# Dealing the row blocks of four matrices over the partitions in turn, in a batched matmul

## The chip, the cores and the metric

The kernel runs on one core of a Trainium2 chip. Time is the device time of one execution in microseconds (us), the median over several executions. A profile also gives TensorE's granted clock, the share of its full clock that it was allowed to run at (1.00 is all of it), and the span, which is the time that the profile covers.

## The reference

```python
b1, b2, m, k, n = 8, 16, 256, 512, 384
x      = randn(b1, b2, m, k)      # float32, 67.1 MB
weight = randn(b1, b2, k, n)      # float32, 100.7 MB
out    = matmul(x, weight)        # float32, 50.3 MB
```

That is 128 separate products of 256x512 by 512x384. Each input is used once, so 218.1 MB have to pass through the DMA queues whatever the kernel does.

## The kernel before

The kernel handles four matrices (G = 4) at a time, 32 groups in all. One load brings the 1,024 rows of four x matrices to 128 partitions, eight consecutive rows (16 KB) to each. With C = 32, partitions 32i to 32i+31 hold matrix i.

```python
e.dma_start(                                   # load
    x_sb[s % XS][:],
    x_rows[bass.ds(n * (G * M), G * M)].rearrange("(p r) k -> p r k", r=R),
).then_inc(x_in[s % XS], 16)
for d in range(G // D):                        # two weight loads of 1.5 MB follow
    ...
```

ScalarE casts x to bf16. TensorE transposes it in pairs of bf16 words, so that in `x_t` the 128 columns (one per partition of x) stand two elements apart. VectorE casts the weights and copies the transposes out of PSUM, the memory that TensorE writes to. Then four matmuls run on four column strips of 32, one for each matrix, each with the 32 columns of its matrix as the stationary operand, which a weight load (LDWEIGHTS in the profile, 4,096 of them beside 4,096 matmuls) brings in before the matmul:

```python
for ko in range(KO):
    for i in range(G):
        mine = slice(i * C, (i + 1) * C)
        ins = e.matmul(
            po[(s * T + q) % PO][mine, rr, :N],
            x_t[s % TS][:, 2 * q + rr, ko // 2, mine, ko % 2],   # stationary
            w_bf[(s * G + i) % WBS][:, ko, :],                   # moving
            start=(ko == 0), stop=(ko == KO - 1),
        )
```

All loads and stores are issued by one queue (SP). Buffers hold two groups of x and of weights and four of the output.

## Time and profile before

| | before |
|---|---|
| time, median | 519.93 us (519.65 to 520.08) |
| DMA packets' share of 16 engines | 99.2% |
| rate in the middle | 425 to 431 GB/s |
| TensorE / VectorE / ScalarE busy | 61% / 62% / 41% |
| one group of four matrices | 15.97 us |

### The profile page before, as it was taken

The numbers are of one execution on the slowest core, as the hardware profiler recorded it, in microseconds if no ns is written. First come the engines' busy times: TensorE is split into PE (matmuls) and PEld (weight loads), VectorE is DVE, ScalarE is ACT, GpSimd is POOL, SyncE is SP. The second block draws the span as 40 slices with busy tenths as digits, with TensorE's granted clock in tenths as the row PEclk, the third lists the DMA queues.
The fourth block names the chain that finished last, engine by engine and source line by source line (L and its number), as shares of the span: only waits on it lengthen the run. The fifth ranks groups of instructions, "written<-read, shape, count | busy, mean of one in ns | idle before, by whom it ended". The sixth has DMA issues, their size and how long they took to land.

```text
span 518.3 us, 11239 instructions
## 1 busy us (share of the span) xinstructions
PE 315.5 (61%) x4608; PEld 198.8 (38%) x4608; DVE 323.9 (62%) x384; ACT 212.7 (41%) x193; POOL 0.7 (0%) x6
## 2 busy tenths in 40 slices
PE   0686773576655675655756557665567665675653
PEld 0455452343433443433424334343344333443331
DVE  0878867655577555775556765557755577555670
ACT  3065462454234553245542445423454324553242
POOL 0000000000000000000000000000000000000000
PEclk9988788877687778678776877778787868886787
DMA  8999999999999999999999999999999999999995
GB/s 332 431 426 426 427 427 429 430 426 429 430 428 429 431 426 428 428 431 431 425 429 429 430 430 429 427 428 429 430 430 428 426 431 430 429 428 427 428 431 214
DMA packets 18868, 218.16 MB, mean 421 GB/s; under 512 B 2096, under 2 KB 2096, under 8 KB 2608
## 3 DMA queue, kind: packets, MB, share of 16 engines
q1 hardware_dynamic: 18864, 218.11, 99.2%
q8 instruction: 2, 0.03, 0.0%
q14 instruction: 2, 0.02, 0.0%
HBM read 167.77 MB, written 50.33 MB: 421 GB/s over the span
## 4 chain that ended last, share of the span: by engine, by line
DMA 81%; DVE 12%; issue 2%; PE 2%; ACT 1%; SPq 0%; DVEq 0%; ACTq 0%
DMA w_sb<-in_weight_dram 81%; DVE w_bf L148 12%; PE po L181 2%; ACT x_bf L130 0%; DVEq _compat.py:109 0%; SPq L108 0%; ACT out_sb L195 0%; SPq L100 0%; DVE x_t L154 0%; DVEq L143 0%; DVEq L230 0%; SPq L107 0%; ACTq L194 0%; SPq L288 0%; SPq L54 0%
## 5 line engine op out<-in xcount | busy, mean ns | idle before, releaser
L148 DVE CAST w_bf<-w_sb 64x1536 bf16<-64x1536 f32 x256 | 244.5, 955 | 179.4 <-DMA w_sb<-in_weight_dram 166.7
L181 PE MATMUL po<-w_bf,x_t 128*32 128x384 bf16 x4096 | 231.4, 400 | 121.0 <-DVE x_t L154 121.0
L195 ACT COPY out_sb<-po 128x768 f32<-128x768 f32 x128 | 99.2, 802 | 290.2 <-PE po L181 290.2
L181 PEld LDWEIGHTS po<-w_bf,x_t 128*32 128x32 bf16 x4096 | 124.5, 117 | 225.4 <-DVE x_t L154 130.9
L167 PE MATMUL pt<-identity,x_bf 128*128 128x128 f32 x512 | 84.0, 329 | 73.0 <-ACT x_bf L130 73.0
L130 ACT CAST x_bf<-x_sb 128x2048 bf16<-128x2048 f32 x64 | 118.4, 1901 | 6.1 <-DMA x_sb<-in_x_dram 6.1
L167 PEld LDWEIGHTS pt<-identity,x_bf 128*128 128x128 f32 x512 | 74.3, 213 | 84.9 <-issue 84.9
L154 DVE COPY x_t<-pt 128x1024 bf16<-128x1024 bf16 x128 | 79.5, 683 | 1.0
L130 ACT ACT_TABLE_LOAD x1 | 1.3, 1283 | 1.3 <-PEq L237 1.3
masks.py:199 POOL TENSOR_SCALAR_AFFINE_SELECT identity<-identity 128x128 f32<-128x128 f32 x1 | 0.3, 292 | 0.2 <-POOL identity L204 0.2
L204 POOL MEMSET identity<- 128x128 f32 x1 | 0.2, 204 | 0.5 <-SPq L54 0.5
L277 POOL MEMSET const-bfloat16-1.0<- 128x1 bf16 x1 | 0.1, 101 | 0.0
L277 POOL MEMSET const-uint8-127<- 128x1 uint8 x1 | 0.1, 101 | 0.0
L277 POOL MEMSET const-float32-0.0<- 128x1 f32 x1 | 0.1, 98 | 0.2 <-issue 0.2
L277 POOL MEMSET const-float32-1.0<- 128x1 f32 x1 | 0.1, 98 | 0.0
## 6 DMA issues: line engine op xcount, KB each, us to landing
w_sb<-in_weight_dram SPq DMA_DIRECT2D x64, 1536.0 KB, 27.5
x_sb<-in_x_dram SPq DMA_DIRECT2D x32, 2048.0 KB, 25.8
out_dram<-out_sb SPq DMA_DIRECT2D x31, 1536.0 KB, 30.6
out_dram<-out_sb SPq DMA_DIRECT2D x4, 384.0 KB, 3.6
```

The source lines that it names most:

```text
L130: ins = e.copy(out=x_bf[s % BS][:, :, h], in_=x_sb[s % XS][:].rearrange("p r (q s c) -> p r s q c", s=S, c=KO)[:, :, h],)
L148: e.tensor_copy(out=w_bf[(s * G + d * D + a) % WBS][h * HP : (h + 1) * HP], in_=w_sb[slot][a * HP : (a + 1) * HP, h * KO : (h + 1) * KO, : ...
L154: e.tensor_copy(out=x_t[s % TS][:, 2 * q : 2 * q + 2], in_=pt[(s * T + q) % PT][:].bitcast(bf16),).then_inc(t_copied, 1)
L167: ins = e.transpose(pt[(s * T + q) % PT][:, rr, h, :], words[:, 2 * q + rr, h :: KO // 2], identity[:],)
L181: ins = e.matmul(po[(s * T + q) % PO][mine, rr, :N], x_t[s % TS][:, 2 * q + rr, ko // 2, mine, ko % 2], w_bf[(s * G + i) % WBS][:, ko, :], ...
L195: e.copy(out=out_sb[s % OS][:, 2 * q : 2 * q + 2, :], in_=po[(s * T + q) % PO][:, :, :N],).then_inc(o_copied, 1)
L204: e.memset(identity[:], 0.0).then_inc(id_done, 1)
L277: nc = _bacc.Bacc("TRN2", target_bir_lowering=False, num_devices=1)
```

## The change

The change deals the row blocks out in turn: partition 4c + i gets block c of matrix i. Every run of four partitions then holds one block of each of the four matrices, and one load reads from four places in HBM at once. So that the results stay in place, a matmul now picks every fourth column. Presumably it was meant to spread the reads.

```diff
         e.dma_start(
-            x_sb[s % XS][:],
-            x_rows[bass.ds(n * (G * M), G * M)].rearrange("(p r) k -> p r k", r=R),
+            x_sb[s % XS][:].rearrange("p r k -> p (r k)"),
+            x_rows[bass.ds(n * (G * M), G * M)].rearrange(
+                "(i c r) k -> c i (r k)", i=G, r=R
+            ),
         ).then_inc(x_in[s % XS], 16)
@@ multiply
-                            x_t[s % TS][:, 2 * q + rr, ko // 2, mine, ko % 2],
+                            x_t[s % TS][:, 2 * q + rr, ko // 2, i::G, ko % 2],
```

## The prediction

> **What bounds the kernel now.** I read the page from the DMA side first, because it has the largest shares: the 40-slice table, the queue table, and the chain that ended last.
>
> ```profile
> DMA  8999999999999999999999999999999999999995
> GB/s 332 431 426 426 427 427 429 430 426 429 430 428 429 431 426 428 428 431 431 425 429 429 430 430 429 427 428 429 430 430 428 426 431 430 429 428 427 428 431 214
> ...
> q1 hardware_dynamic: 18864, 218.11, 99.2%
> ...
> DMA 81%; DVE 12%; issue 2%; PE 2%; ACT 1%; SPq 0%; DVEq 0%; ACTq 0%
> ```
>
> The second row is the rate in each fortieth of the span (13 us): a ramp at 332, a flat 425 to 431 GB/s, a tail at 214. The queue line says that packets filled 99.2% of 16 engines' 518.3 us. The chain agrees: 81% of it is a transfer. The transfers are not late for want of requests: in the table of issues a weight load lands 27.5 us after it is issued, although its 1.5 MB at 429 GB/s need 3.7 us. So about 27 us of work is queued ahead of it.
>
> No view lists single packets, so I summed the trace's packet records by size. There are 4,096 packets of 16 KB, which are the x loads (32 loads x 128 partitions), with a median of 611 ns and a 99th percentile of 627 ns. There are 12,160 packets of 12 KB (weights and stores) with a median of 460 ns. Per engine that is 157.7 us for x, 351.4 us for 12 KB packets, 3.9 us for the last stores' 3 KB packets and 1.2 us for semaphores: 514.2 us of 518.3. The time is this sum plus a start and an end.
>
> Next the compute side, in the groups by line and in one group of the timeline (columns there: start, length, engine, line, work, count, idle before):
>
> ```profile
> L181 PE MATMUL po<-w_bf,x_t 128*32 128x384 bf16 x4096 | 231.4, 400 | 121.0 <-DVE x_t L154 121.0
> L181 PEld LDWEIGHTS po<-w_bf,x_t 128*32 128x32 bf16 x4096 | 124.5, 117 | 225.4 <-DVE x_t L154 130.9
> ```
>
> ```profile
> 254.25 7.86 DVE L148 CAST w_bf<-w_sb 64x1536 bf16<-64x1536 f32 x8 [5.55 <-DMA w_sb<-in_weight_dram]
> ...
> 255.66 3.11 PE L167 MATMUL pt<-identity,x_bf 128*128 128x128 f32 x16 [1.98 <-ACT x_bf L130]
> ...
> 262.14 2.48 DVE L154 COPY x_t<-pt 128x1024 bf16<-128x1024 bf16 x4
> 262.88 0.14 PEld L181 LDWEIGHTS po<-w_bf,x_t 128*32 128x32 bf16 x8 [4.52 <-DVE x_t L154]
> 262.89 7.28 PE L181 MATMUL po<-w_bf,x_t 128*32 128x384 bf16 x128 [4.12 <-DVE x_t L154]
> ...
> 266.70 3.07 PEld L181 LDWEIGHTS po<-w_bf,x_t 128*32 128x32 bf16 x76 [0.16 <-issue]
> ```
>
> A group of four matrices takes 15.97 us (in the chain the weight casts start at 206.39, 238.33 and 270.27, two groups apart). VectorE waits 5.55 us for the weights' DMA, then PE waits for VectorE. Were data always there, PE's loop would be 3.1 (transposes) + 0.75 (first copy, 262.14 to 262.89) + 7.3 (matmuls) = 11.2 us, VectorE's 7.9 + 2.5 = 10.3 us. Compute has 4.8 us to spare per group.
>
> One thing in the last row matters later: 76 weight loads in 3.07 us are one per 40 ns, back to back. In that stretch (granted clock 0.99) weight loading is full; earlier in the same phase (clock 0.50) four loads fill 0.16 of every 0.32 us.
>
> [...] Before, both sides count 128. After, the source counts 32 (c) outermost and the destination 128[...]. No run here shows the new shape yet.[...] The new x load puts successive partitions 512 KiB apart[...]. The transposed x columns were read at a 4 B step[...] and will be read at 16 B[...]. The trace of before has no such read, so it cannot confirm the penalty.
>
> **The change part by part.**
> *x load.* It removes nothing: 32 loads of 2 MB, still one contiguous 16 KB row block per partition, so still 4,096 packets of 16 KB. What moves is which block each partition gets: partition 4c+i now has block c of matrix i, where partition 32i+c had it. Only the HBM addresses change. Cost per engine: 256 packets x 611 ns = 156.4 us, unchanged if the memory keeps up. Before, the engines read blocks of the same 2 MB, only in another order, and 99% of the packets were within 16 ns of the floor; HBM showed no strain. I take an allowance of 0 to 3 ns per packet in the mean, 256 x 3 = 0.8 us at most, centre 0.3 us. The three-dimensional source may cost SP a little more at each issue than the present 0.33 us, but behind a 27 us backlog only the very first issue shows: 0.2 us as a guess.
>
> *Matmuls.* Same number of instructions in the same order on every engine (I compared the two builds), same 32 columns and 384 moved elements. The picked columns come out as matrix i's rows in order, so the output rows and stores are as before. Only the weight-load step grows.[...] I bound it: at worst[...] the pace doubles, from 40 to an estimated 80 ns. In the slow-clock part four loads then need just the 0.32 us there are: no change. In the fast part 0.16 us per four becomes 0.32 us. A steady group gets 76 x 40 ns = 3.0 us longer: 11.2 + 3.0 = 14.2 us, still under 15.97. Nothing of that reaches the end time.
>
> *The tail.* This is the one place where matmul time is on the path. The chain of waits ends with:
>
> ```profile
> 502.57 6.94 PE po L181 x128
> ```
>
> After it come one 0.80 us copy and one 384 KB store. 88 of its 128 weight loads run at the fast pace (3.66 us in the timeline); at 80 ns they take 7.0 us, so +3.4 us on the end; with half of the penalty (60 ns) it is +1.6 us. I give no penalty, half and the whole equal chances: (0 + 1.6 + 3.4)/3 = +1.7 us expected, less some 0.5 us because the stores of the last groups, still queued until about 511 us, hide a part of it: +1.2 us.
>
> Sum: 519.9 + 0.3 (HBM) + 0.2 (first issue) + 1.2 (tail) = 521.6; the outcome without any penalty, 520.4, is the most probable single one, so I settle a little lower, at 521.2.
>
> **The rivals.**
> *A: PE takes over as the bound.* The matmul phase may grow to 15.97 - 3.1 - 0.75 = 12.1 us, that is 95 ns per weight load, before the DMA queue starves. For: the loads are already back to back at 40 ns. Against: they would have to slow 2.4-fold. At 120 ns a group would take 3.85 + 128 x 0.12 = 19.2 us, and 32 groups some 615 us. Chance 3%.
>
> *B: HBM slows the x packets.* For: four streams 512 KiB apart[...]. Against: each read is still 16 KB long,[...] and the packet times of before sit on their floor with one core alone on its memory.[...] At 10%, 536 us. Chance of over 2% from here: 2%.
>
> *C: the engines share the work worse*[...]. For: a new shape that the trace hasn't shown.[...] With x at half rate: +157 us, 677 us. Chance 2%.
>
> *D: it gains.* Spreading x over four matrices could be meant to feed HBM better. Against:[...] Over 2% would need 10.4 us; 1% as a chance for a cause not thought of.
>
> **How range and chances follow.** Unchanged kernels repeat within 519.65 to 520.08. Below 519 only rival D leads. Upwards, a doubled weight load gives about 523.8[...]. So 519.0 to 525.0 should hold it 8 times in 10. Rivals A, B and C sum to 0.07 for slower by over 2% (above 530); rest 0.92.
>
> **What would show each step right or wrong.** Right: the GB/s row again at 425 to 431 with q1 near 99%, 4,096 packets of 16 KB with a median of 611 ns, and VectorE still waiting for the weights' DMA before each other group. The weight-load rows of the timeline tell the step's price: 0.16 us per four means no penalty, up to 0.32 us in the fast part the penalty, and the last matmul phase would read 6.9 us or up to 10.3 us. Wrong: a GB/s row that falls (B or C; packets slower everywhere is B, uneven or doubled ones C), or DMA tenths below 9 in the middle with VectorE waiting for PE (A).

## The result

The changed kernel takes 520.36 us (520.20 to 520.53, four runs) against 519.98 us. The ratio is 1.0009 with a 95% interval of 0.9994 to 1.0024. A ratio is the mean time of one kernel's fast runs over that of the other's in the same rounds, so it is not quite the ratio of the medians quoted beside it.

The profile after, first the table of slices, the queue line and the chain by engine:

```profile
DMA  8999999999999999999999999999999999999995
GB/s 337 427 427 426 418 428 429 435 424 429 428 427 431 428 427 430 429 428 431 426 429 426 432 430 427 426 431 429 428 430 431 427 429 431 428 428 426 429 430 219
...
q1 hardware_dynamic: 18864, 218.11, 99.1%
...
DMA 80%; DVE 12%; issue 2%; PE 2%; ACT 1%; SPq 0%; DVEq 0%; ACTq 0%
```

Little moved here. The one slice that stands out is the fifth, with 418 GB/s where the kernel before has 427; more on it below. In the packet records, the 4,096 packets of 16 KB are still there, with a median of 611 ns as before. The sums per engine are 157.1 us for x (157.7 before), 351.7 us for the 12 KB packets (351.4), 3.9 and 1.2 us for the rest: 513.9 us against 514.2. Which engine moved a packet is not recorded: "per engine" means the sum divided by 16.

The groups by line (busy us, mean ns of one, idle time before and its releaser):

```profile
L183 PE MATMUL po<-w_bf,x_t 128*32 128x384 bf16 x4096 | 238.5, 408 | 122.4 <-DVE x_t L156 122.4
L183 PEld LDWEIGHTS po<-w_bf,x_t 128*32 128x32 bf16 x4096 | 157.6, 148 | 200.3 <-DVE x_t L156 130.4
```

The mean weight load has gone from 117 to 148 ns and weight-load busy time from 124.5 to 157.6 us. This is the largest visible price of the change, 33 us of work, and the time does not show it. The same group of the timeline as before (start, length, engine, line, work, count, idle before):

```profile
254.45 7.86 DVE L150 CAST w_bf<-w_sb 64x1536 bf16<-64x1536 f32 x8 [5.43 <-DMA w_sb<-in_weight_dram]
...
256.36 2.84 PE L169 MATMUL pt<-identity,x_bf 128*128 128x128 f32 x16 [1.99 <-ACT x_bf L132]
...
262.34 2.48 DVE L156 COPY x_t<-pt 128x1024 bf16<-128x1024 bf16 x4
263.09 7.36 PEld L183 LDWEIGHTS po<-w_bf,x_t 128*32 128x32 bf16 x128 [4.29 <-DVE x_t L156]
263.09 7.70 PE L183 MATMUL po<-w_bf,x_t 128*32 128x384 bf16 x128 [3.89 <-DVE x_t L156]
```

VectorE still waits over 5 us for the weights, and TensorE for VectorE. The weight loads now merge into one row of 7.36 us, where before they stood as blocks of 0.16 us. Merged rows mislead, though. They join pieces with small gaps between them, and that is how I misread the row "3.07 ... x76" of before. Busy time by window is the honest view. Its columns are the window, its length, then busy us with counts for PE, weight loads, VectorE, ScalarE, GpSimd, then granted clock, DMA share and GB/s. This is one fast stretch before:

```profile
266.70:270.20 3.50, 3.46 (x84) 1.98 (x76) 0.00 (x0) 2.58 (x3) 0.00 (x0) 0.99 1.00 421
```

and the same window after, where the granted clock was 0.84:

```profile
266.70:270.20 3.50, 3.50 (x80) 2.74 (x76) 0.00 (x0) 1.98 (x3) 0.00 (x0) 0.84 1.02 432
```

76 weight loads kept the loader busy for 1.98 of 3.50 us before and 2.74 after. It was never full. The instruction records say why: at the fast clock the four loads of a block start within some 20 ns of each other, last 97 ns each, and the next four start 162 ns after the first four. After the change each lasts 137 ns or a little more, and the blocks are still 162 ns apart. The matmuls set the pace, in both kernels.

The second small difference is on the queue that issues the DMAs. A line of the x tile's view before (durations min/median/max in ns):

```profile
L100 SPq DMA_DIRECT2D x_sb<-in_x_dram x32: 327/333/703, 1.0 to 463.6; - x32
```

and after:

```profile
L100 SPq DMA_DIRECT2D x_sb<-in_x_dram x32: 545/566/661, 1.0 to 464.2; - x32
```

An issue of the new load takes 0.23 us more. 27 us of work are queued, so I expected only the very first issue to matter. The first packet starts at 2.40 us after the span's start instead of 1.99. The packets make up for that at once, though, and lose something later. The same columns as above, first before:

```profile
0.00:4.00 4.00, 0.00 (x0) 0.00 (x0) 0.00 (x0) 1.28 (x1) 0.70 (x6) 1.00 0.55 131
62.00:66.00 4.00, 3.99 (x100) 2.29 (x92) 3.01 (x4) 3.35 (x4) 0.00 (x0) 1.00 0.99 418
```

and after:

```profile
0.00:4.00 4.00, 0.00 (x0) 0.00 (x0) 0.00 (x0) 1.28 (x1) 0.70 (x6) 1.00 0.41 139
62.00:66.00 4.00, 2.62 (x68) 2.08 (x56) 3.15 (x4) 3.93 (x3) 0.00 (x0) 1.00 1.01 390
```

In the first 4 us the changed kernel starts as many bytes as the other, and a few more: the first 64 packets last 717 ns in the mean instead of 859. Between 62 and 66 us it falls behind: the 12 KB packets that start from 62.5 to 65.0 us last 537 ns in the mean instead of 466. Against packets of the usual length (611, 460 and 121 ns), the surplus per engine is 0.5 us smaller than before in the first 8 us, and 0.3 us larger from 60 to 68 us.

The last matmul phase, on the chain that ended last, after the change:

```profile
502.67 7.42 PE po L183 x116
```

It is 0.48 us longer than the 6.94 us of before, yet the span is only 0.06 us longer (518.40 against 518.34). The profiled run of before, at 520.11 us, is one of the slower ones of its kernel, so this is weak evidence that the chain does not set the end. In the packet records of before there is something stronger. 12 KB packets follow each other without a gap until 512.48 us, and 3 KB packets, one each 118 ns, until 516.28. I read this row as one engine that works through its 12 KB store packets and then its 32 packets of 3 KB; the records name no engine. It reaches the last piece only at 515.3 us, although that piece was issued at about 510.4.

### The profile page after: what moved, and what is told of

Read it like the earlier page. It is cut to its first block, busy times and chain, and to the rows that moved or that the text cites. A ratio compares the mean times of both kernels' runs of the same rounds, so it can differ in the third digit from the quotient of the medians.

```text
span 518.4 us, 11239 instructions
## 1 busy us (share of the span) xinstructions
PE 315.7 (61%) x4608; PEld 227.0 (44%) x4608; DVE 323.9 (62%) x384; ACT 213.1 (41%) x193; POOL 0.7 (0%) x6
## 2 busy tenths in 40 slices
DMA packets 18868, 218.16 MB, mean 421 GB/s; under 512 B 2096, under 2 KB 2096, under 8 KB 2608
## 3 DMA queue, kind: packets, MB, share of 16 engines
q1 hardware_dynamic: 18864, 218.11, 99.1%
## 4 chain that ended last, share of the span: by engine, by line
DMA 80%; DVE 12%; issue 2%; PE 2%; ACT 1%; SPq 0%; DVEq 0%; ACTq 0%
DMA w_sb<-in_weight_dram 80%; DVE w_bf L150 12%; PE po L183 2%; ACT x_bf L132 1%; DVEq _compat.py:109 0%; SPq L100 0%; SPq L110 0%; ACT out_sb L197 0%; DVE x_t L156 0%; DVEq L145 0%; SPq L109 0%; DVEq L232 0%; ACTq L196 0%; SPq L290 0%; SPq L54 0%
## 5 line engine op out<-in xcount | busy, mean ns | idle before, releaser
L183 PE MATMUL po<-w_bf,x_t 128*32 128x384 bf16 x4096 | 238.5, 408 | 122.4 <-DVE x_t L156 122.4
L183 PEld LDWEIGHTS po<-w_bf,x_t 128*32 128x32 bf16 x4096 | 157.6, 148 | 200.3 <-DVE x_t L156 130.4
L169 PE MATMUL pt<-identity,x_bf 128*128 128x128 f32 x512 | 77.3, 310 | 71.9 <-ACT x_bf L132 71.9
L169 PEld LDWEIGHTS pt<-identity,x_bf 128*128 128x128 f32 x512 | 69.4, 211 | 82.4 <-issue 82.4
```

What stands on the lines that cost most here:

```text
L169: ins = e.transpose(pt[(s * T + q) % PT][:, rr, h, :], words[:, 2 * q + rr, h :: KO // 2], identity[:],)
L183: ins = e.matmul(po[(s * T + q) % PO][mine, rr, :N], x_t[s % TS][:, 2 * q + rr, ko // 2, i::G, ko % 2], w_bf[(s * G + i) % WBS][:, ko, :], ...
```

## The experiments

**Theory 1:** the span is the first packet's start (2.0 us), plus 514 us of packets on an engine, plus a fixed 2 us at the end. The stride costs nothing, and a first issue of the long kind costs 0.4 us. **Theory 2:** the chain is right and the last matmul phase, which the stride lengthens, is on the path.

### The changed kernel once more

> The changed kernel once more, beside the kernel before on the same chip, as the yardstick for the three runs with it. Theory 1 (the time is first packet + packet time + a fixed end): the first DMA packet starts 0.4 us later than before (2.4 against 2.0 us), the packet sum is the same within 0.5 us, so 520.3 to 520.5 us, ratio 1.0005 to 1.0010. Theory 2 (the tail's matmul phase is on the path, as the chain says): also about +0.5 us, from the last phase being 7.4 instead of 6.9 us. Rival 3 (chance): ratio 1.0000 within its interval.

It measured 520.29 us (520.23 to 520.43) beside 520.01 us for the kernel before (519.73 to 520.28), ratio 1.0006, interval 0.9992 to 1.0019. The interval contains 1, so these times alone do not settle 0.3 us. The first packet started at 2.45 us, and the rate from 62 to 66 us is 387 GB/s.

### The x load alone

The diffs from here on are shortened to the lines that matter.

```diff
 the changed load, and
-                            x_t[s % TS][:, 2 * q + rr, ko // 2, i::G, ko % 2],
+                            x_t[s % TS][:, 2 * q + rr, ko // 2, mine, ko % 2],
```

> Only the x load is changed; the columns are picked as before, so the rows of the four matrices are mixed and the result is wrong on purpose. Theory 1: carries the whole of the difference, 520.3 to 520.5 us, with the first x issue at 0.66 instead of 0.39 us on the sync engine and the first packet at 2.4 us. Theory 2: 519.9 to 520.0 us, as before. Rival B of the prediction (HBM minds the new order): x packets longer than 611 ns in the median and more than +0.5 us.

It measured 520.30 us (520.25 to 520.40). The result is wrong, as intended. The first packet started at 2.41 us, and x packets have a median of 611 ns. The groups by line show weight loads at their old length:

```profile
L183 PEld LDWEIGHTS po<-w_bf,x_t 128*32 128x32 bf16 x4096 | 123.7, 116 | 225.3 <-DVE x_t L156 131.6
```

So the new load carries the whole of the small difference, without any slower weight load. Its rate from 62 to 66 us is 381 GB/s, so the slow packets come with the load too.

### The column pick alone

```diff
 the load of before, and
-                            x_t[s % TS][:, 2 * q + rr, ko // 2, mine, ko % 2],
+                            x_t[s % TS][:, 2 * q + rr, ko // 2, i::G, ko % 2],
```

> Only the columns are picked with stride four; the x load is as before; wrong result on purpose. Weight loads last some 137 to 142 ns instead of 97 ns as in the changed kernel. Theory 1: 519.9 to 520.0 us, ratio 1.0000, because the last DMA packets end after the matmuls have long been passed by queued stores. Theory 2: +0.5 us, 520.4 us. My prediction's step: up to +1.2 us.

It measured 520.04 us (519.94 to 520.16), ratio 1.0000, interval 0.9987 to 1.0014. The result is wrong as intended. The weight loads are long:

```profile
L181 PEld LDWEIGHTS po<-w_bf,x_t 128*32 128x32 bf16 x4096 | 157.2, 147 | 196.5 <-DVE x_t L154 130.4
```

The profiled run happened to have a last matmul phase of 7.95 us, a full 1.0 us longer than before, yet its span was 518.26 us. That speaks against theory 2, but one phase of varying length in one profile is a weak control. A designed one follows further down.

### Weights first

This is the changed kernel, correct, with one reordering:

```diff
 def load(e, t, U, s):
+    first = n == 0                      # only the very first group
-    load x; load weights
+    if not first: load x
+    load weights
+    if first: load x
```

> The changed kernel, correct, with the first group's two weight loads issued before its x load, so that the first issue is of the short kind again. Theory 1: the first packet is back at 2.0 us and the time at 519.9 to 520.0 us. Theory 2: 520.4 us, since the tail is untouched. Either way the first cast of x comes some 7 us later, which costs nothing if the DMA engines are what bounds the kernel.

It measured 519.98 us (519.79 to 520.06), ratio 0.9998. The first packet is back at 1.99 us. No run of it overlaps with a run of the changed kernel (520.20 and up), so the new order gives back what the change had cost. It matches the kernel before and does not beat it.

It does not show that the first packet's start was the cost. The reordering removes the slow stretch as well: from 62 to 66 us the rate is 421 GB/s, against 390, 387 and 381 in the three profiles with the new load in front. By the packet records the 0.41 us at the front had been made up by 4 us, and the loss came at 62 to 66 us. What makes those packets slow stays open. The 512 KiB run further down has the same dip (390 GB/s), but it also has a faster start than any of these (176 GB/s in the first 4 us). Nor was the kernel before run with its weights first, which would show whether the order gains something by itself.

### The last copy delayed

The kernel before, correct. The extra copies go to a spare buffer, so that they do not touch the output.

```diff
+    spare = sbuf("spare", [P, 2, 2, N], fp32, 1)[0]
@@ copy_out
+        if isinstance(n, int) and n == NG - 1 and q == T - 1:
+            for twice in range(2):
+                e.copy(out=spare[:, twice], in_=po[(s * T + q) % PO][:, :, :N])
```

> The kernel before, correct, with two extra copies of the last output piece to a spare buffer put in front of the last copy, so that the last store is issued some 1.6 us (2 x 0.80) later. In the trace of before one DMA engine works through queued stores without a break to the end at 516.3 us and starts on the last piece only at 515.3 us, while that piece is issued at about 510.4. Theory 1 (that engine sets the end): no change, 519.9 to 520.1 us. Theory 2 (the chain of waits: last matmuls, last copy, last store set the end): +1.6 us, 521.6 us, ratio 1.003.

It measured 519.92 us (519.68 to 520.11) against 519.89 us, ratio 1.0002, interval 0.9988 to 1.0015. ScalarE's rows at the end of this run's timeline:

```profile
509.18 1.50 ACT L198 COPY spare<-po 128x768 f32<-128x768 f32 x2 [0.50 <-PE po L182]
510.56 0.82 ACT L202 COPY out_sb<-po 128x768 f32<-128x768 f32 x1
```

The last copy ended at 511.38 us, 1.05 us later than in the profile of before, although the matmuls of this run were a little earlier. The last packet ended at 515.95 us, 0.3 us earlier. The delay vanished, so the last copy is not on the path, and theory 2 is out. The packet records fit the other reading: a DMA engine's backlog sets the end (12 KB packets without a gap until 512.48 us, the last packet at 516.28 us in the profile of before). Of theory 1 this confirms the end; its account of the start did not hold (see the weights first).

### Without the DMA bound: the column step alone

To see what the stride costs where TensorE has less slack, I cut the loads. From the fifth group on, each load fetches one row per partition, so the queue is only 63% full. The result is wrong. Four kernels differ in the step between the picked columns:

```diff
 4 bytes:   x_t[...][:, 2*q + rr, ko//2, mine, ko % 2]
+8 bytes:   x_t[...][:, 2*q + rr, ko//2, 64*(i//2) + i%2 : 64*(i//2) + 64 : 2, ko % 2]
+16 bytes:  x_t[...][:, 2*q + rr, ko//2, i::G, ko % 2]
+32 bytes:  x_t[...][:, 2*q + rr] as (p, 256 columns, 2), [:, 4*(ko//2) + i :: 8, ko % 2]
```

> The kernel before with its loads cut: from the fifth group on each load fetches one row per partition only, so that the DMA engines no longer bound it; wrong result on purpose. It shows the compute floor: 11.2 us per group by my prediction's working (3.1 + 0.75 + 7.3), some 32 x 11.2 + 20 = 380 us[...]. Columns at a 4-byte step: a weight load lasts 97 ns in the fast part.

> As the run with the 4-byte step, but the columns at an 8-byte step[...].[...] If the cost grows with the step: between 97 and 140 ns.

> As the run with the 4-byte step, but with the change's 16-byte step. My prediction's step (weight loads back to back, one per 40 ns, pace doubled): +3.0 us per group, some +96 us. What the profile after suggests (four loads run side by side on four column groups; 140 ns still fits into the 162 ns that four matmuls take): within 2% of the run at 4 bytes.

> As the run with the 4-byte step, but the columns at a 32-byte step.[...] if it grows with the distance, over 162 ns and then the pace of the matmuls breaks: four per 200 ns or more, over 10% longer.

| step | time, two runs | median weight load | usual matmul phase (median) |
|---|---|---|---|
| 4 B | 364.27 us | 97 ns | 5.385 us |
| 8 B | 363.75 us | 107 ns | 5.399 us |
| 16 B | 364.87 us | 137 ns | 5.428 us |
| 32 B | 365.39 us | 139 ns | 5.429 us |

The lines of the groups by line, for 4 bytes:

```profile
L186 PEld LDWEIGHTS po<-w_bf,x_t 128*32 128x32 bf16 x4096 | 109.5, 100 | 89.2 <-DVE x_t L159 27.8
```

and for 16 bytes:

```profile
L186 PEld LDWEIGHTS po<-w_bf,x_t 128*32 128x32 bf16 x4096 | 149.8, 139 | 50.4 <-DVE x_t L159 30.4
```

A load of 32 columns takes 40 ns longer at 16 bytes than at 4. At 32 bytes it takes only 2 ns more than that, so from 16 to 32 bytes the price hardly grows with the distance. Why it levels off is not shown. The phase grows by 0.043 us, which is about one load's 40 ns. That fits a first block with nothing to hide behind and later ones that fit into 162 ns. Over 32 groups it would be 1.4 us. These times cannot tell: the four values lie within 1.64 us, 16 bytes are 0.60 us over 4 bytes, and two runs of the 4-byte kernel differ by 1.34 us (363.60 and 364.94). The 96 us that my prediction's step would give are ruled out. The first row of each page says what bounds them; for 4 bytes:

```profile
PE 262.2 (72%) x4608; PEld 182.8 (50%) x4608; DVE 324.5 (89%) x384; ACT 212.6 (59%) x193; POOL 0.7 (0%) x6
```

VectorE is, at 7.86 + 2.48 = 10.3 us of a 10.4 us group (its copies start at 206.19 and 216.60). So in such a group the stride is not on the path even here.

### HBM: all 128 partitions 512 KiB apart

```diff
-            x_rows[bass.ds(n * (G * M), G * M)].rearrange("(p r) k -> p r k", r=R),
+            x_rows.rearrange("(p n r) k -> p n (r k)", p=P, r=R)[:, bass.ds(n, 1), :]
+                .rearrange("p n e -> p (n e)"),
```

> The hard form of rival B: the kernel before, but each x load takes one 16 KB block from every one of the 128 matrices, so that all 128 partitions lie exactly 512 KiB apart in HBM (the changed kernel has only four such streams); wrong result on purpose. If HBM has room to spare with one core at work: x packets still 611 ns, 520 us.[...]

It measured 519.99 us against 519.87 us, ratio 1.0002, interval 0.9985 to 1.0019. The median of the x packets is 611 ns. Their mean after the first 20 us is 614.5 ns against 612.1 before, and the 99th percentile of all of them 734 against 627. A few packets do take longer, but with the faster start it costs nothing that the time shows. As a cost of several microseconds, rival B is ruled out even with 128 streams at that distance, where the change has four.

### Another outer count: 16

```diff
-                "(i c r) k -> c i (r k)", i=G, r=R        # 32 outer, 4 inner
+                "(i c r) k -> c i (r k)", i=8, r=R        # 16 outer, 8 inner
 and the columns picked as before
```

> Rival C, first form: the x load deals eight half matrices (128 row blocks as 16 outer by 8), columns picked as before; wrong result on purpose. The source's slowest dimension is 16[...]. If only the number of engines matters: 520 us, as before.[...] x packets of up to 1,220 ns, up to 677 us.

It measured 683.65 us (681.16 and 686.14), ratio 1.3151. Its page:

```profile
GB/s 244 300 289 254 268 328 320 293 298 338 348 342 301 300 319 352 352 311 305 300 346 349 339 299 304 328 349 346 309 303 301 355 351 324 300 306 331 349 358 343
...
q1 hardware_dynamic: 18864, 218.11, 100.0%
```

The queue is full: its packets fill 100.0% of the span of 16 engines. The semaphore packets are 2,096, as before, 16 for each of 131 transfers. But x packets take 1,253 ns in the median instead of 611. Their sum per engine is 304 us instead of 158, and 12 KB packets lose 23 us beside them. This is rival C's case, x at half rate, one number away from the change. The run shows that the time of an x packet doubles (1,253 ns against 611) when the outer count falls from 32 to 16, with as many semaphore packets for a transfer as before. The order of the addresses in HBM changes as well; the 512 KiB run makes that an unlikely cause but is not the same pattern. Why the packets take twice as long is not shown, and no record here names the engine of a packet.

### Another outer count: 8

```diff
+                "(i c r) k -> c i (r k)", i=16, r=R       # 8 outer, 16 inner
```

> Rival C, second form: dealt over 16 quarters (8 outer by 16); wrong result on purpose.[...] 512 x 611 ns + 356 us = 670 us of packets each; time some 675 us, with the queue's share of 16 engines near 76%.[...]

It measured 997.73 and 1,157.71 us. The second is the profiled run and is slow, and I don't explain the difference between the two. The profile page counts fewer packets:

```profile
DMA packets 18613, 218.16 MB, mean 189 GB/s; under 512 B 1841, under 2 KB 1841, under 8 KB 2353
```

There are 1,840 semaphore packets in the queue instead of 2,096, which is 256 less, or 8 less for each of the 32 x loads. If each engine at work on a load adds one, the 8 that are left of 16 mean that x ran on 8 engines. That is an estimate from these counts, since no record names the engines. My 675 us was far too low, because I had halved the engines (an estimate: 512 packets on each instead of 256) but left the packets at 611 ns. In the profiled run their median is 1,648 ns. If both prices apply, half the engines and half the rate, x takes 4 x 157.7 = 631 us, and with 356 us of other packets an estimate of 987 us comes out, near the 998 us of the faster run. The sum fits, but it shows no cause. It also leaves out that in the profiled, slow run the 12 KB packets took longer too (566 us per engine instead of 351).

## Why the prediction was right, and which of its steps were not

- **The bound, and the x packets:** right. The same packets at the same 611 ns fill the same queue. The packet sum fell by 0.3 us: the first packets were 0.5 us shorter per engine, those at 60 to 68 us 0.3 us longer. The latter has the size of my allowance for HBM, but whether HBM causes it is not shown. Even 128 streams 512 KiB apart cost nothing visible in the time (519.99 against 519.87 us).
- **The first issue, +0.2 us as a guess:** right that the first packet starts later, by 0.41 us, but not shown to be a cost. The new load carries the 0.3 to 0.4 us between the kernels, and with the weights first they go. Yet the packets had made up the late start by 4 us, and the loss shows at 62 to 66 us. Why it arises there stays open.
- **Weight loads "back to back", "weight loading is full", pace doubled to 80 ns:** wrong. I took a merged row of the timeline for busy time. Four loads run side by side, they last 97 ns, and there was a spare 65 ns in each 162 ns. The change took 40 of them. That the load would get slower was right (117 to 148 ns in the mean); that its pace would follow was not, and the doubling was an estimate of mine. So rival A's threshold of 95 ns per load is not a measure of anything either: the loads already lasted longer than that.
- **The tail, +1.2 us:** wrong, and more so than its size. I took the chain for the path. The chain ends in the last matmuls, copy and store because each releases the next, but by my reading of the packet records the last store then waits behind one DMA engine's backlog. A last copy 1.05 us later left the end where it was. The sentence that queued stores hide "a part of it" should have been the whole step.
- **The compute floor of 11.2 us per group:** 10.4 us when measured. TensorE's clock was higher in that run (0.934 in the mean, against 0.787 in the profile of before) and its phases shorter (5.4 us of matmuls instead of 7.3), and VectorE's 10.3 us become the bound. The conclusion, several microseconds to spare, holds.
- **Rival C, 2%:** it did not happen here, but no trace had shown how an outer count of 32 would do, so 2% was an estimate without a run behind it. With an outer count of 16 the kernel takes 683.65 us.

The sum of 521.2 us was 0.8 us too high: 0.4 us of real cost stood against 1.3 us expected above 519.9. That the 520.4 us given for "no penalty" came so close is luck in part: its 0.3 and 0.2 us were an allowance and a guess. The range held since everything that the steps got wrong was small beside the DMA time.

## What to carry to other kernels

When a queue is full, add up its packets first: start, packet sum, end. Here, what left packet count, packet time and the queue's share (99.2% and 99.1%) alone did not move the time, and the chain of waits pointed at work that the queue's backlog hid. A later first packet is not a loss by itself (0.41 us were made up by 4 us here): compare the bytes moved some microseconds on. Before dealing rows over partitions in a DMA, look at the outermost count of the source: 32 kept the rate here (packets of 611 ns), 16 doubled the time of those packets (1,253 ns), and 8 brought them to 1,648 ns in a slow run, with half the semaphore packets of those loads. Read how full a unit is from busy time in a window, never from a merged timeline row.
